# Exponents of the gated DeltaNet from one stacked product, one lane transpose for four, and the low halves of 22 weight tiles made a stage earlier and kept in DRAM

## The chip, the cores and the metric

The kernel runs on one core of one Trainium2 chip. The metric is device time in microseconds, the median of several executions. The engines are PE (TensorE: matmuls, and transposes as matmuls), DVE (VectorE), ACT (ScalarE), POOL (GpSimd) and SP, whose queue issues every DMA of this kernel. PEld is the loading of PE's stationary operand.

## The reference

Two layers over 256 latent and 256 context tokens of width 1024. Layer 0 mixes tokens with an RG-LRU block, layer 1 with a gated DeltaNet; a SwiGLU feed-forward part follows each. Every part is normed and modulated by six vectors made from `silu(c) @ ada_w`. Cut to the DeltaNet step, which is where most of the change lies (the kernel takes chunks of 128 tokens where this takes 64):

```python
def step(s, xs):
    qc, kc, vc, gc, bc = xs
    gc = jnp.cumsum(gc, axis=-1)
    diff = gc[..., :, None] - gc[..., None, :]
    decay = jnp.where(incl, jnp.exp(jnp.where(incl, diff, 0.0)), 0.0)
    kb = kc * bc[..., None]
    m = jnp.where(strict, jnp.einsum('bhid,bhjd->bhij', kb, kc) * decay, 0.0)
    rhs = jnp.concatenate([vc * bc[..., None], kb * jnp.exp(gc)[..., None]], axis=-1)
    sol = lax.linalg.triangular_solve(m, rhs, left_side=True, lower=True, unit_diagonal=True)
    ...
    attn = jnp.where(incl, jnp.einsum('bhid,bhjd->bhij', qc, kc) * decay, 0.0)
```

It runs for 16 value heads (8 key heads, each used by two), in two directions, over context and latents. `decay` is a 128x128 matrix for each chunk, direction and head: exp of a difference of two running sums. The projections `h @ w_in` in front of it are products with 49 weight tiles of 128 columns (8 q, 8 k, 16 v, 16 z and one of small rows).

## The kernel before

**Products.** A weight tile (128x1024 floats, 512 KB) is loaded into `raw` (three buffers), rounded to a high half `whi`, and what is left over becomes the low half `wlo` (two buffers each): `weight` (L704). A product (`product`, L943) is then three matmuls for each of 8 contraction tiles: high by high, high by low of the input, low by high. The copy to `whi` goes to ACT or DVE, the subtraction that makes `wlo` to DVE or POOL; inside the DeltaNet stage, until the z tiles, the subtraction is given to POOL alone. So a tile is 24 matmuls, 512 columns wide with both token sets.

**Stages.** In order: the RG-LRU part (to about 240 us of the profile), the feed-forward part of layer 0 (`ffn`, L1099, about 240 to 640), the DeltaNet (about 640 to 1130 with its output product, `ps_wo`), the feed-forward part of layer 1. In the first feed-forward part a background list `cur["bg"]` makes the modulation vectors of layer 1: each `bg_step` (L781) records one step, which loads a 512 KB tile into one of two `ring` slots and adds it on DVE to `acc`. `product` records one such step each time.

**DeltaNet.** Heads are taken in four groups of two key heads (four value heads), numbered 0 to 3. `stage_a` (A) projects one key head: k, two v tiles, q. For a group, `stage_e` (E) makes the exponents (`exponents`, L1275) and their exp, the 32 decay matrices of the tile `gn`; `stage_n` (N) multiplies them by k k^T, transposes the four 32x32 diagonal blocks into lanes (L1417) and inverts them there in a loop of 60 dependent DVE operations (`lmul`, `lw`); `stage_l` (L) assembles the whole inverse with small matmuls (`ps_w`, `ps_z`); `stage_p` (P) makes the attention matrices `at`, with exponents of its own (`ps_a`); `stage_c` (C) runs the chunks. Z makes the z tiles, W the output product that can start early.

An exponent tile of 128x512 (four heads) is a sum in one PSUM bank of three matmuls: a column term, whose stationary operand `cT` has 64 rows and whose moving operand `pick` is a broadcast; a row term (`rows`, `own`), and a mask (`below`, `identr`). In `stage_p` the column term of the second direction has 128 rows instead (`npick`, `rT`). There are 8 such tiles in each E and 4 in each P: 48 in all.

**Order.** Nothing is issued in the order of the code. A recorder collects the operations of a stage and `flush` (L391) places them with a list scheduler: every operation has a priority (its place in the record plus a bias), costs and latencies written in the source, and buffers are granted as they come free. The DeltaNet's record follows the table `PROG` (L73), its biases `TUNE["bias"]`. Each engine then runs its own list strictly in order, SP's list of DMAs included: a DMA whose buffer is not free holds back every DMA behind it. PE matmuls of any stage may stand between others.

Of the kernel before, what the change touches and what calls it, by code (L numbers as in the profile page):

```python
# [42 lines left out]
def _shuffle(sh, pattern, sizes):  # L43
# [18 lines left out]
    for g, n in zip(lhs, sh.shape, strict=True):  # L62
# [3 lines left out]
        for a in g:  # L66
# [6 lines left out]
PROG = "A0 A1 E0 A2 N0 A3 E1 L0 P0 N1 C0 A4 A5 E2 P1 L1 N2 C1 A6 Z0 A7 E3 L2 P2 N3 Z1 C2 Z2 Z3 L3 W0 P3 C3"  # L73
TUNE = dict(warm=5000, ev=3000, stay=(300, 0), g0=4, early=(1, 2, 4, 6), eb=0, ea=(0, 1, 1, 1), nwo=2, prog=PROG,
            bias={'C3': -1500, 'N0': 100, 'N': -700, 'Z3': -1200, 'L': -1500, 'E3': 700, 'W': 10000, 'L3': -800, 'E': -300, 'W0': 10000, 'P': -100, 'E0': -300, 'N3': -700, 'P2': 0, 'C': 400, 'A': 700, 'Z': 700, 'C1': 0})
# [545 lines left out]
def hybrid_block(ctx: ExitStack, tc: tile.TileContext, I, out, dbg=None):  # L621
# [82 lines left out]
    def weight(*src, cols=1024, aside=False, place=None):  # L704
# [29 lines left out]
    def ada_steps(l, m, direct=False):  # L734
# [41 lines left out]
        yield  # L776

# [165 lines left out]
    def product(src, n_k, xs, n, wmap=lambda w, k: w[:, 128 * k:128 * k + 128]):  # L943
        wh, wl = early.pop(0) if early else weight(src)
# [154 lines left out]
    def ffn(l, n, upd, hh, hl, first=None):  # L1099
# [32 lines left out]
    ada_later(1, 0, 1, 2, 3, 4, 5)  # L1132
# [114 lines left out]
    id64 = piece(64)  # L1247
    V.tensor_tensor(id64, ident[:, 0:64], ident[:, 64:128], OP.add)
    npick = dn.tile([128, 64], F32R, name="npick")
    V.tensor_scalar(npick, id64, -1.0, None, OP.mult)  # L1250
    pick = dn.tile([128, 32], F32R, name="pick")
    V.tensor_tensor(pick[0:64], ident[0:64, 0:32], ident[0:64, 32:64], OP.add)
    mod4 = piece(4)
    V.tensor_reduce(out=mod4, in_=ident.rearrange("p (m h) -> p h m", h=4), axis=AX.X, op=OP.add)
    own = {}
    for sign in (1, -1):
        own[sign] = dn.tile([128, 16], F32R, name=f"own{sign + 1}")
        t = piece(16)
        V.tensor_reduce(out=t, in_=id64.rearrange("p (i h) -> p i h", h=4), axis=AX.X, op=OP.add)
        V.tensor_scalar(own[sign], t, float(sign), None, OP.mult)  # L1260
    gch = dn.tile([128, 2, 2, 4, 16], F32R, name="gch")
    for d in range(2):
        R.copy(gch[:, d, 0], gc[:, :, d, :])
        V.tensor_tensor(gch[:, d, 1], gc[:, :, d, :], gch[:, d, 0].bitcast(F32), OP.subtract)
    pt = bank("tr", "ps_gt")
    for d in range(2):
        T.transpose(pt[:, 128 * d:128 * d + 128], gch[:, d].rearrange("p a c h -> p (a c h)").bitcast(F32), ident)
    rT = dn.tile([128, 2, 128], F32R, name="rT")
    R.copy(rT, pt[:, 0:256].rearrange("p (d i) -> p d i", d=2))
    rows = []  # L1270
    for d in range(2):
        rows.append(dn.tile([128, 4, 128], F32R, name=f"rows{d}"))
        V.tensor_tensor(rows[d], rT[:, d].bitcast(F32).rearrange("p (o i) -> p o i", o=1).to_broadcast([128, 4, 128]),
                        mod4.rearrange("p (h o) -> p h o", o=1).to_broadcast([128, 4, 128]), OP.mult)
# [35 lines left out]
    def stage_a(h):  # L1310
        a = A[h] = {}

        ps = product(I["dn_w_in"][8 + h], NK, hx1, 512) if h else ps_k0
# [18 lines left out]
        for j in range(2):  # L1332
            ps = product(I["dn_w_in"][16 + 2 * h + j], NK, hx1, 512)
# [23 lines left out]
    def stage_e(g):  # L1357
# [14 lines left out]
        cb = dn.tile([128, 2, 32], F32R, tag="cb", bufs=2, name="cb")  # L1372
        lf = lb.rearrange("p c d h -> p (c d h)")
        V.tensor_copy(cb[:, 0], lf)
        V.tensor_tensor(cb[:, 1], lf, cb[:, 0].bitcast(F32), OP.subtract)
        pt = bank("tr", "ps_cb")
        T.transpose(pt[0:64, 0:128], cb.rearrange("p a s -> p (a s)").bitcast(F32), ident)
        cT = t["cT"] = dn.tile([128, 128], F32R, tag="cT", bufs=2, name="cT")
        V.tensor_copy(cT[0:64], pt[0:64, 0:128])
        for c in range(4):  # L1380
            for d in range(2):
                s = sidx(c, d, 0)
                p4 = exponents(g, c, d, (1, -1)[d], 1, column(t, c, d), [gn])
                S.activation(gn[:, s:s + 4, :], p4, AF.Exp)

    def column(t, c, d):
        return t["cT"][0:64], pick[0:64, 4 * (2 * c + d):4 * (2 * c + d) + 4], 64

    def stage_n(g):
# [138 lines left out]
    def stage_p(g):  # L1528
# [3 lines left out]
        for c in range(2):  # L1532
            for d in range(2):
                col = (rT[:, 1], npick[:, 16 * (2 + c) + 4 * g:16 * (2 + c) + 4 * g + 4], 128) if d else column(t, 2 + c, 0)
                p4 = exponents(g, 2 + c, d, 1, (1, -1)[d], col, t["at"], "ps_a")
                for q in range(2):
                    S.activation(t["at"][q][:, c, d], p4[:, 2 * q:2 * q + 2], AF.Exp)
# [296 lines left out]
```

## Time and profile before

| | |
|---|---|
| median of 3 executions | 1363.38 us (1362.26 to 1370.28) |
| profiled execution: its time, its span | 1364.68 us, 1363.0 us |
| mean granted TensorE clock | 0.976 |
| PE busy, PEld busy | 1308.6 us, 1110.3 us |
| DVE, ACT, POOL busy | 1035.0, 564.9, 229.6 us |
| DMA moved, mean rate | 195.60 MB, 144 GB/s |

A row of the profile names what an instruction writes and reads (`ps_mm<-hh,whi`: the PSUM bank `ps_mm` from the operands `hh` and `whi`). All calls pass one helper, so all rows have line L612 and are told apart by these names. Matmuls are pipelined: the duration of one is longer than its distance to the next, so PE's real price for a matmul is the distance between the starts of neighbours. Instructions of PE in float32 (not in the rounded form) leave two records each.

### The profile page before, as it was taken

The page shows a single profiled execution, that of the slowest core. Times are in us where ns is not written, and L with a number is a line of the kernel's source. Part 1 is how long each engine was busy: PE and PEld are TensorE (multiplying, and loading weights), DVE is VectorE, ACT ScalarE, POOL GpSimd, SP SyncE. Part 2 cuts the span into 40 slices and gives each one's busy share as a digit, 9 for nine tenths or more (in the row PEclk, how much of TensorE's full clock was granted, in tenths as well). Part 3 has the DMA queues.
Part 4 walks back from the last instruction along what each step waited for, and adds up shares of the span by engine and source line. Part 5 has one row for each costly group of instructions (what it writes and reads, how often), then busy time and mean ns, then how long its engine had stood idle before and what let it go on. Part 6 is the DMA issues. An engine that isn't in the chain of part 4 may idle for free.

```text
span 1363.0 us, 23260 instructions
## 1 busy us (share of the span) xinstructions
PE 1308.6 (96%) x9200; PEld 1110.3 (81%) x9200; DVE 1035.0 (76%) x1851; ACT 564.9 (41%) x1053; POOL 229.6 (17%) x203
## 2 busy tenths in 40 slices
PE   5999999899999999999998999999998998999997
PEld 3677778878888888888867788898798888999997
DVE  5799986988775665557868889798499376877775
ACT  3388773444321111005746656747646431211100
POOL 2000000110100001212524333334243100000000
PEclk9899999899999999999999999999999699999999
DMA  9545423365564665333523222323133025455563
GB/s 352 197 165 188 140 94 114 124 202 196 188 228 164 192 208 183 98 110 125 178 74 129 71 78 79 105 71 121 63 117 117 25 92 180 139 182 180 179 181 116
DMA packets 61261, 195.60 MB, mean 144 GB/s; under 512 B 6752, under 2 KB 9952, under 8 KB 60896
## 3 DMA queue, kind: packets, MB, share of 16 engines
q1 hardware_dynamic: 61152, 194.12, 42.8%
q8 instruction: 72, 1.18, 0.4%
q14 instruction: 37, 0.30, 0.1%
HBM read 184.13 MB, written 9.96 MB: 142 GB/s over the span
## 4 chain that ended last, share of the span: by engine, by line
PE 56%; issue 15%; DVE 6%; ACT 4%; DMA 1%; POOL 0%; POOLq 0%; SPq 0%; ACTq 0%; DVEq 0%
PE ps_mm L612 29%; PE ps_dn L612 9%; PE ps_e L612 2%; PE ps_wo L612 2%; PE ps_y L612 2%; PE ps_w L612 2%; PE ps_z L612 2%; PE ps_s L612 1%; DVE lw L612 1%; PE ps_ks L612 1%; DVE cu L612 1%; PE ps_a L612 1%; PE ps_qs L612 1%; PE ps_o L612 1%; ACT gn L612 1%
## 5 line engine op out<-in xcount | busy, mean ns | idle before, releaser
L612 PE MATMUL ps_mm<-hh,whi 128*128 128x512 f32 (+1 forms) x888 | 327.4, 370 | 8.0 <-DVE cu L612 5.6
L612 PE MATMUL ps_mm<-hl,whi 128*128 128x512 f32 (+1 forms) x888 | 327.3, 370 | 0.9 <-DVE hl L612 0.8
L612 PE MATMUL ps_mm<-hh,wlo 128*128 128x512 f32 (+1 forms) x888 | 326.2, 368 | 1.7 <-POOL wlo L612 1.7
L612 DVE TENSOR_TENSOR wlo<-raw,whi 128x1024 fp32r<-128x1024 f32 (+2 forms) x183 | 220.5, 1205 | 17.4 <-ACT whi L612 8.3
L612 DVE CAST whi<-raw 128x1024 fp32r<-128x1024 f32 (+2 forms) x177 | 120.2, 679 | 145.8 <-PE ps_mm L612 81.0
L612 POOL TENSOR_TENSOR wlo<-raw,whi 128x1024 fp32r<-128x1024 f32 x55 | 132.0, 2402 | 506.5 <-DVE whi L612 351.3
L612 PEld LDWEIGHTS ps_mm<-hh,whi 128*128 128x128 f32 x888 | 169.6, 191 | 40.6 <-issue 9.9
L612 PEld LDWEIGHTS ps_mm<-hh,wlo 128*128 128x128 f32 x888 | 169.7, 191 | 29.6 <-POOL wlo L612 2.4
L612 PEld LDWEIGHTS ps_mm<-hl,whi 128*128 128x128 f32 x888 | 170.0, 192 | 27.4 <-DVE hl L612 2.0
L612 PE MATMUL ps_dn<-fh,wlo 128*128 128x256 f32 (+1 forms) x374 | 122.7, 328 | 0.0
L612 PE MATMUL ps_dn<-fl,whi 128*128 128x256 f32 (+1 forms) x374 | 122.5, 327 | 0.0
L612 PE MATMUL ps_dn<-fh,whi 128*128 128x256 f32 (+1 forms) x374 | 122.2, 327 | 0.0
L612 PE MATMUL ps_mm<-h2h,whi 128*128 128x256 f32 x352 | 100.4, 286 | 1.1 <-ACT h2h L612 1.1
L612 PE MATMUL ps_mm<-h2l,whi 128*128 128x256 f32 x352 | 100.6, 286 | 0.5 <-DVE h2l L612 0.3
L612 PE MATMUL ps_mm<-h2h,wlo 128*128 128x256 f32 x352 | 100.1, 284 | 0.0
L612 ACT ACTIVATE whi<-raw 128x1024 fp32r<-128x1024 f32 (+2 forms) x61 | 63.2, 1036 | 77.8 <-PE ps_mm L612 45.1
L612 ACT ACTIVATE fh<-sg 128x256 fp32r<-128x256 f32 (+1 forms) x43 | 22.4, 522 | 156.4 <-DVE sg L612 156.3
L612 ACT ACT_TABLE_LOAD x59 | 75.7, 1283 | 7.0 <-DMA sm<-small 3.4
L612 PEld LDWEIGHTS ps_dn<-fl,whi 128*128 128x128 f32 x374 | 71.1, 190 | 6.4 <-issue 0.4
L612 PEld LDWEIGHTS ps_dn<-fh,wlo 128*128 128x128 f32 x374 | 71.1, 190 | 6.4 <-issue 0.4
L612 PEld LDWEIGHTS ps_dn<-fh,whi 128*128 128x128 f32 x374 | 71.1, 190 | 6.0
L612 DVE SCALAR_TENSOR_TENSOR x<-ring,cs,x 128x1024 f32<-128x1024 f32 x49 | 63.9, 1304 | 15.4 <-DMA ring<-ada_w 14.4
(326 smaller groups left out, 2544.7 us busy)
## 6 DMA issues: line engine op xcount, KB each, us to landing
ring<-ada_w SPq DMA_DIRECT2D x96, 512.0 KB, 4.5
raw<-ffn_gu SPq DMA_DIRECT2D x88, 512.0 KB, 3.5
raw<-dn_w_in SPq DMA_DIRECT2D x49, 512.0 KB, 3.5
raw<-ffn_down SPq DMA_DIRECT2D x34, 512.0 KB, 3.6
raw<-rg_w_in SPq DMA_DIRECT2D x16, 512.0 KB, 4.5
raw<-ffn_down SPq DMA_DIRECT2D x17, 384.0 KB, 3.4
raw<-dn_w_out SPq DMA_DIRECT2D x12, 512.0 KB, 3.6
raw<-rg_w_out SPq DMA_DIRECT2D x10, 512.0 KB, 3.4
```

Source lines behind the costliest of these rows:

```text
L612: call(*[real(x) for x in args], **{n: real(v) for n, v in kw.items()})
```

## The change

**Stacked exponents.** The column and the row term become one matmul. For each group a tile `src` holds, side by side, high and low halves of the running sums, ones, and the column logarithms; three transposes put them on partitions (`ps_src`), and DVE multiplies them into two operands by masks of zeros and ones (`spread`): `X` (four heads, 128x512, shared by all exponents of the group) and `Y` (eight chunk and direction pairs, 128x1024), with `Y2` (128x256) for the second direction of P. An exponent tile is then X by one block of Y, and the mask: two matmuls, both over 128 rows. `X`, `Y`, `Y2` and `src` have one buffer each, so the next group's E writes them after this group's P has read them. The old operands (`cT`, `rows`, `own`, `npick`, `rT`) go.

**One lane transpose.** Four copies on ACT gather the diagonal blocks into `lc` (32 partitions by 1024 each), and one DVE transpose of 128x1024 takes the place of four of 32x1024.

**Low parts in DRAM.** `low_steps` adds 22 background steps in the feed-forward part of layer 0, between the second and the third modulation vector of layer 1. Each loads one k or v tile of the DeltaNet into a `ring` slot, rounds it on ACT, subtracts (DVE or POOL), and writes the 512 KB of low half to DRAM. For these tiles `weight` later makes only `whi`; `wlo` is loaded from DRAM. The feed-forward loop records one more background step in every second round.

**Order.** `PROG` moves P before the next E and some other entries; the bias of L goes from -1500 to -2200.

On PE, the first two exponent tiles of group 0 before, with the products around them (`ps_e` the exponents, `ps_mm` a projection):

```order
L612 MATMUL ps_mm<-hh,whi 128x512
L612 MATMUL ps_e<-pick,cT 128x512
L612 MATMUL ps_e<-rows_5410,own_5116 128x512
L612 MATMUL ps_e<-below,identr 128x512
L612 MATMUL ps_mm<-hl,whi 128x512
L612 MATMUL ps_e<-pick,cT 128x512
L612 MATMUL ps_e<-rows_5417,own_5118 128x512
L612 MATMUL ps_e<-below,identr 128x512
```

The same place now (`ex` is X, `ey` is Y):

```order
L612 MATMUL ps_mm<-hh,whi 128x512
L612 MATMUL ps_e<-ex,ey 128x512
L612 MATMUL ps_e<-below,identr 128x512
L612 MATMUL ps_mm<-hl,whi 128x512
L612 MATMUL ps_e<-ex,ey 128x512
L612 MATMUL ps_e<-below,identr 128x512
```

One matmul of three has gone from each tile, and none of those left works on 64 rows.

On SP, in the feed-forward part of layer 0, a stretch before (`raw<-ffn_gu` is the next product's weight tile, `ring` the background's):

```order
L612 DMA raw<-ffn_gu 128x1024
L612 DMA ring<-ada_w 128x1024
L612 DMA raw<-ffn_gu 128x1024
L612 DMA ring<-ada_w 128x1024
L612 DMA raw<-ffn_gu 128x1024
L612 DMA ring<-ada_w 128x1024 x2
L612 DMA raw<-ffn_gu 128x1024
```

And a stretch now, while the low parts are made:

```order
L612 DMA low<-ring 128x1024 x2
L612 DMA ring<-dn_w_in 128x1024
L612 DMA raw<-ffn_gu 128x1024
L612 DMA ring<-dn_w_in 128x1024
L612 DMA raw<-ffn_gu 128x1024
L612 DMA low<-ring 128x1024 x2
L612 DMA ring<-dn_w_in 128x1024
L612 DMA raw<-ffn_gu 128x1024
```

There are eleven such pairs of writes, most with this pattern after them: two loads of the ring and two weight tiles between one pair and the next. Each ring load needs the write that empties its slot to have landed, and a weight tile stands behind it.

On DVE, the lane transposes of group 0 before, between the convolutions (`cu`) of a projection:

```order
L612 STREAM_TRANSPOSE lw<-gn 32x1024
L612 SCALAR_TENSOR_TENSOR cu<-ps_mm,sm,cu 128x2x254
L612 STREAM_TRANSPOSE lw<-gn 32x1024
L612 SCALAR_TENSOR_TENSOR cu<-ps_mm,sm,cu 128x2x255
L612 TENSOR_SCALAR cu<-ps_mm,sm 128x512
L612 SCALAR_TENSOR_TENSOR cu<-ps_mm,sm,cu 128x2x255
L612 SCALAR_TENSOR_TENSOR cu<-ps_mm,sm,cu 128x2x254
L612 STREAM_TRANSPOSE lw<-gn 32x1024
```

And now:

```order
L612 SCALAR_TENSOR_TENSOR cu<-ps_mm,sm,cu 128x2x255
L612 TENSOR_SCALAR cu<-ps_mm,sm 128x256
L612 STREAM_TRANSPOSE lw<-lc 128x1024
L612 SCALAR_TENSOR_TENSOR cu<-ps_mm,sm,cu 128x254
L612 MEMSET lw 128x32
```

One transpose stands where four stood, and the convolutions are no longer parted by several of them.

```diff
-PROG = "A0 A1 E0 A2 N0 A3 E1 L0 P0 N1 C0 A4 A5 E2 P1 L1 N2 C1 A6 Z0 A7 E3 L2 P2 N3 Z1 C2 Z2 Z3 L3 W0 P3 C3"
+PROG = "A0 A1 E0 A2 N0 A3 P0 E1 L0 N1 A4 A5 C0 P1 E2 L1 N2 C1 A6 Z0 A7 P2 E3 L2 Z1 N3 C2 Z2 Z3 L3 W0 P3 C3"
...
     def weight(*src, cols=1024, aside=False, place=None, low=None):
         r = raws.pop(0) if raws else raw_load(src, cols)
         hi, lo = place or (wp.tile([128, 1024], F32R, tag=t, bufs=NB[t], name=t) for t in ("whi", "wlo"))
+        if low is not None:
+            R.copy(hi, r)
+            sync.dma_start(out=lo.bitcast(F32), in_=low)
+            return hi, lo
...
+    def low_steps(tiles):
+        low = dr.tile([len(tiles), 128, 1024], F32, name="low")
+        for n, i in enumerate(tiles):
+            r, hi = next(cur["araw"]), cur["acc"][:, 1]
+            sync.dma_start(out=r, in_=I["dn_w_in"][i], after=cur["late"])
+            S.activation(hi.bitcast(F32R), r, AF.Copy)
+            R.tt(r.bitcast(F32R), r, hi, OP.subtract)
+            sync.dma_start(out=low[n], in_=r)
+            LOW[i] = low[n]
+            yield
...
+                bg_step(l == 0 and j % 2)
...
-    ada_later(1, 0, 1, 2, 3, 4, 5)
+    ada_later(1, 0, 1)
+    cur["bg"].append(low_steps([i for h in range(NQK) for i in (8 + h, 16 + 2 * h, 17 + 2 * h)][2:2 + TUNE["low"]]))
+    ada_later(1, 2, 3, 4, 5)
...
-    def exponents(g, c, d, sign, bound, col, to, name="ps_e"):
-        ps = bank("tr", name)
-        p4 = ps.rearrange("p (h i) -> p h i", h=4)
-        i = 4 * c + g
-        lhs, rhs, n = col
-        T.matmul(p4, lhs, rhs.rearrange("p (h o) -> p h o", o=1).to_broadcast([n, 4, 128]), start=True, stop=False, needs=to)
-        T.matmul(p4, own[sign][:, i:i + 1].to_broadcast([128, 128]), rows[d], start=False, stop=False)
+    def exponents(lhs, rhs, bound, to, name):
+        p4 = bank("tr", name).rearrange("p (h i) -> p h i", h=4)
+        T.matmul(p4, lhs, rhs, start=True, stop=False, needs=to)
         lhs, rhs = (identr, below) if bound > 0 else (below, identr)
         T.matmul(p4, lhs, rhs.rearrange("p (o i) -> p o i", o=1).to_broadcast([128, 4, 128]), start=False, stop=True)
...
+        for k, i in enumerate((0, 1, 3)):
+            T.transpose(pt[:, 128 * k:128 * k + 128], src[:, i:i + 2].rearrange("p a x -> p (a x)").bitcast(F32), ident,
+                        needs=[X, Y, Y2])
+        spread(X, pt[:, 0:128], mod4, 4)
+        spread(Y, pt[:, 128:256], own, 8)
+        spread(Y2, pt[:, 256:384], own2, 2)
...
+        lc = dn.tile([128, 32, 32], F32, tag="lane", bufs=3, name="lc")
         w = dn.tile([128, 32, 32], F32, tag="lane", bufs=3, name="lw")
         for b in range(4):
             r = slice(32 * b, 32 * b + 32)
-            V.transpose(w[r], gn[r, :, 32 * b:32 * b + 32].rearrange("p s f -> p f s"))
+            S.activation(lc[r], gn[r, :, 32 * b:32 * b + 32], AF.Copy)
+        V.transpose(w, lc.rearrange("p s f -> p f s"))
```

More of the change, by code (lines that the diff above doesn't have):

```diff
@@ L702, in raw_load, with weight @@
         return r
-    def weight(*src, cols=1024, aside=False, place=None):
+    def weight(*src, cols=1024, aside=False, place=None, low=None):
         r = raws.pop(0) if raws else raw_load(src, cols)
         hi, lo = place or (wp.tile([128, 1024], F32R, tag=t, bufs=NB[t], name=t) for t in ("whi", "wlo"))
+        if low is not None:
+            R.copy(hi, r)
+            sync.dma_start(out=lo.bitcast(F32), in_=low)
+            return hi, lo
         if aside:
@@ L776, in ada_steps @@
         yield
+    LOW = {}
+    def low_steps(tiles):
[8 more added lines that the diff above has]
+            yield
     def ada_later(l, *ms, direct=False):
@@ L941, in hybrid_block, with product @@
     ol = m0.tile([128, NK, 512], F32R, name="ol", tag="ol", bufs=1)
-    def product(src, n_k, xs, n, wmap=lambda w, k: w[:, 128 * k:128 * k + 128]):
-        wh, wl = early.pop(0) if early else weight(src)
+    def product(src, n_k, xs, n, wmap=lambda w, k: w[:, 128 * k:128 * k + 128], low=None):
+        wh, wl = early.pop(0) if early else weight(src, low=low)
         bg_step()
@@ L1246, in hybrid_block @@
     R.copy(identr, ident)
[L1247 to L1253, printed above, removed]
-    V.tensor_reduce(out=mod4, in_=ident.rearrange("p (m h) -> p h m", h=4), axis=AX.X, op=OP.add)
[L1255 to L1274, printed above, removed]
-    def exponents(g, c, d, sign, bound, col, to, name="ps_e"):
-        ps = bank("tr", name)
-        p4 = ps.rearrange("p (h i) -> p h i", h=4)
-        i = 4 * c + g
-        lhs, rhs, n = col
-        T.matmul(p4, lhs, rhs.rearrange("p (h o) -> p h o", o=1).to_broadcast([n, 4, 128]), start=True, stop=False, needs=to)
-        T.matmul(p4, own[sign][:, i:i + 1].to_broadcast([128, 128]), rows[d], start=False, stop=False)
+    sel = dn.tile([128, 14], F32, name="rowsel")
@@ new lines, in hybrid_block @@
+    mod4, own, own2 = sel[:, 0:4], sel[:, 4:12], sel[:, 12:14]
+    V.tensor_reduce(out=mod4, in_=ident.rearrange("p (m h) -> p h m", h=4), axis=AX.X, op=OP.add)
+    mod32 = piece(32)
+    V.tensor_reduce(out=mod32, in_=ident.rearrange("p (m h) -> p m h", h=4), axis=AX.X, op=OP.add)
+    V.tensor_reduce(out=own, in_=mod32.rearrange("p (x i) -> p i x", i=8), axis=AX.X, op=OP.add)
+    V.tensor_scalar(own[0:64, 1:8:2], own[0:64, 1:8:2], -1.0, None, OP.mult)
+    V.tensor_scalar(own2, own[:, 5:8:2], -1.0, None, OP.mult)
@@ L1283, in exponents, with spread @@
+    def spread(out, part, mask, n):
+        V.tensor_tensor(out, part.rearrange("p (o i) -> p o i", o=1).to_broadcast([128, n, 128]),
+                        mask.rearrange("p (n o) -> p n o", o=1).to_broadcast([128, n, 128]), OP.mult)
+    def exponents(lhs, rhs, bound, to, name):
+        p4 = bank("tr", name).rearrange("p (h i) -> p h i", h=4)
+        T.matmul(p4, lhs, rhs, start=True, stop=False, needs=to)
         lhs, rhs = (identr, below) if bound > 0 else (below, identr)
@@ L1311, in stage_a @@
         a = A[h] = {}
-        ps = product(I["dn_w_in"][8 + h], NK, hx1, 512) if h else ps_k0
+        ps = product(I["dn_w_in"][8 + h], NK, hx1, 512, low=LOW.get(8 + h)) if h else ps_k0
         kT = a["kT"] = dn.tile([128, 512], F32, tag="kT", bufs=8, name="kT")
@@ L1332, in stage_a @@
         for j in range(2):
-            ps = product(I["dn_w_in"][16 + 2 * h + j], NK, hx1, 512)
+            ps = product(I["dn_w_in"][16 + 2 * h + j], NK, hx1, 512, low=LOW.get(16 + 2 * h + j))
             v2 = conv_silu(ps, 16 + 2 * h + j, 2)
@@ L1382, in stage_e @@
                 s = sidx(c, d, 0)
[L1383 to L1387, printed above, removed]
+                S.activation(gn[:, s:s + 4, :], exponents(Y[:, 2 * c + d], X, 1, [gn], "ps_e"), AF.Exp)
     def stage_n(g):
@@ L1533, in stage_p @@
             for d in range(2):
-                col = (rT[:, 1], npick[:, 16 * (2 + c) + 4 * g:16 * (2 + c) + 4 * g + 4], 128) if d else column(t, 2 + c, 0)
-                p4 = exponents(g, 2 + c, d, 1, (1, -1)[d], col, t["at"], "ps_a")
+                lhs = t["Y2"][:, c] if d else t["Y"][:, 4 + 2 * c]
+                p4 = exponents(lhs, t["X"], (1, -1)[d], t["at"], "ps_a")
                 for q in range(2):
```

25 lines of the change are left out of this document (16 added, 9 removed).

## The prediction

> **What bounds the kernel now.** I read the page's busy shares and chain of waits first.
>
> ```profile
> span 1363.0 us, 23260 instructions
> PE 1308.6 (96%) x9200; PEld 1110.3 (81%) x9200; DVE 1035.0 (76%) x1851; ACT 564.9 (41%) x1053; POOL 229.6 (17%) x203
> PE 56%; issue 15%; DVE 6%; ACT 4%; DMA 1%; POOL 0%; POOLq 0%; SPq 0%; ACTq 0%; DVEq 0%
> ```
>
> PE is busy nearly throughout and the chain of what ended last lies mostly on it; POOL and SP's queue hold none. Next I took the table of busy times by stretch, for the feed-forward part (240 to 640 us), the DeltaNet (640 to 1130), and places in it.
>
> ```profile
> core 0: us, PE busy (x) PEld busy (x) DVE busy (x) ACT busy (x) POOL busy (x), PEclk, DMA share, GB/s
> 0.00:25.00 25.00, 12.93 (x72) 8.15 (x72) 11.70 (x32) 7.88 (x20) 3.20 (x20) 1.00 0.91 331
> 240.00:640.00 400.00, 394.67 (x1942) 328.56 (x1941) 279.66 (x351) 102.34 (x155) 45.37 (x28) 0.99 0.52 170
> 640.00:1130.00 490.00, 470.52 (x4292) 401.21 (x4290) 387.01 (x921) 288.86 (x614) 164.70 (x135) 0.97 0.29 96
> 710.00:720.00 10.00, 5.16 (x30) 4.46 (x30) 9.87 (x14) 3.74 (x5) 4.76 (x2) 0.93 0.26 87
> 850.00:950.00 100.00, 98.05 (x1073) 85.57 (x1072) 88.45 (x196) 63.35 (x138) 39.13 (x38) 1.00 0.30 101
> 1050.00:1075.00 25.00, 22.49 (x419) 20.13 (x417) 9.89 (x15) 14.32 (x28) 5.81 (x5) 0.56 0.17 54
> ```
>
> Both long stretches are PE's: 394.67 of 400 us and 470.52 of 490. In the DeltaNet DVE is second with 79%, up to 88% between 850 and 950; ACT and POOL have room. So PE's own work there is worth time until DVE takes over.
>
> **The exponents.** The timeline of PE at the first exponents of group 0 gives start and duration of each matmul:
>
> ```profile
> 682.65 0.48 PE L612 MATMUL ps_e<-pick,cT 64*128 64x512 f32 x1
> 683.06 0.50 PE L612 MATMUL ps_e<-rows,own 128*128 128x512 f32 x1
> 683.40 0.40 PE L612 MATMUL ps_e<-below,identr 128*128 128x512 f32 x1
> 683.73 0.48 PE L612 MATMUL ps_e<-pick,cT 64*128 64x512 f32 x1
> ...
> 684.48 0.40 PE L612 MATMUL ps_e<-below,identr 128*128 128x512 f32 x1
> 684.71 0.39 PE L612 MATMUL ps_mm<-hh,wlo 128*128 128x512 f32 x1
> 684.94 0.40 PE L612 MATMUL ps_mm<-hh,whi 128*128 128x512 f32 x1
> ...
> 675.28 0.28 PE L612 MATMUL ps_mm<-hh,wlo 128*128 128x256 f32 x1
> 675.40 0.28 PE L612 MATMUL ps_mm<-hh,whi 128*128 128x256 f32 x1
> ...
> 675.64 0.38 PE L612 MATMUL ps_a<-npick,rT 128*128 128x512 f32 x1
> 675.86 0.28 PE L612 MATMUL ps_mm<-hh,wlo 128*128 128x256 f32 x1
> 675.97 0.39 PE L612 MATMUL ps_a<-rows,own 128*128 128x512 f32 x1
> 676.20 0.28 PE L612 MATMUL ps_mm<-hh,whi 128*128 128x256 f32 x1
> ```
>
> A tile with `pick` takes 683.73 - 682.65 = 1.08 us from start to start; a plain 512-column matmul takes 684.94 - 684.71 = 0.23, the mask too (684.71 - 684.48). The surplus of 0.4 us sits at the change between 64 and 128 rows: after `npick`, which has 128 rows, the same two steps take 0.22 and 0.23. X and Y have 128 rows, so I price the new tile as two plain matmuls, 0.46. Counts: 32 tiles in E and 8 in P lose 1.08 - 0.46 = 0.62 each, 24.8 us; 8 tiles in P lose the 0.22 of `npick`, 1.8 us. Sum 26.6. The other end is that only the streaming goes: 48 x 0.23 = 11.0. I take 26.6, since the `npick` rows show the plain price in the same place.
>
> The Trainium skill speaks of a lower price: "TensorE: Matmul & The Clock Gate", section "Back-to-back issue gap", gives about 131 ns per 512-column matmul in a sustained stream. By it 48 matmuls would be an estimated 6 us; the rows here show 0.23 us for a plain one and more at a change of rows.
>
> New on PE are 12 transposes of 128x128 for six of the old kernel. Rows for transposes, copies and subtractions, from the groups by form and the answer for one tile:
>
> ```profile
> L612 PE MATMUL ps_vt<-ident,cu x64: 271/273/332, 652.8 to 958.6; 128*128 128x128 f32 x64
> L612 DVE STREAM_TRANSPOSE lw<-gn 32x1024 f32<-32x1024 f32 x16 | 32.0, 2001 | 0.3
> L612 DVE STREAM_TRANSPOSE ld<-lw 128x1024 f32<-128x1024 f32 x4 | 8.2, 2050 | 0.1
> L612 DVE TENSOR_TENSOR at<-ps_kq,at 128x512 f32<-128x512 f32 x16 | 10.3, 679 | 0.2 <-PE ps_kq L612 0.2
> L612 DVE TENSOR_TENSOR wlo<-raw,whi 128x1024 fp32r<-128x1024 f32 x162 | 201.5, 1244 | 14.7 <-ACT whi L612 7.2
> L612 ACT ACTIVATE whi<-raw 128x1024 fp32r<-128x1024 f32 x57 | 60.3, 1057 | 73.7 <-PE ps_mm L612 45.1 <-issue 17.2 <-PE ps_dn L612 7.6
> L612 POOL TENSOR_TENSOR wlo<-raw,whi 128x1024 fp32r<-128x1024 f32 x55 | 132.0, 2402 | 506.5 <-DVE whi L612 351.3 <-ACT whi L612 104.4 <-PE ps_mm L612 28.2
> ```
>
> Six more at 0.27 at most: +1.6; pipelined they are nearer to +0.7. I take +1.
>
> **The spreads and the lane transpose.** A spread has no row. The nearest is `at<-ps_kq,at`, two operands with one in PSUM, 0.68 us for 512 elements; X, Y and Y2 are 1792, so 3.5 x 0.68 = 2.4 us a group, 9.5 in all. Sixteen lane transposes of 2.00 us go (32.0) and four of 2.05 come (8.2): a transpose costs the same on 32 partitions as on 128. DVE in the DeltaNet has 32.0 - 8.2 - 9.5 = 14.3 us less, the small operations that leave and come taken as equal. ACT gets 16 copies of 1024 elements, at 1.06 each 17 us, on 289 of 490: hidden. On a path that ends something stands only the N of group 3, where its L and C follow with little else for PE: 4 x 2.0 = 8.0 us become 4 x 1.06 + 2.05 = 6.3. Bounds -3 and +3 (ACT's copies queue behind others); I take -1. In group 0 the row of 710 to 720 shows PE at 5.16 of 10 while DVE is full: those 4.8 us could shrink, and I put them in a rival, not in the sum, since what DVE does next there is the convolution, which stays.
>
> **The low parts, in the feed-forward part.** Per tile: a ring load, an ACT copy (1.06), a subtraction (1.24 on DVE), a 512 KB write. 22 of them are 23 us of ACT on 102 of 400 and 27 us of DVE on 280, covered by PE's 394.67. The traffic rises by 23 MB on 400 us, 58 GB/s on 170; 331 were moved in the first stretch. What can fail is the pace of the ring. From the DMA views (time to landing, medians; the first three rows of 240 to 640, the others of 640 to 1130 and of the whole):
>
> ```profile
> ring<-ada_w SPq DMA_DIRECT2D x56, 512.0 KB, 4.4
> raw<-ffn_gu SPq DMA_DIRECT2D x41, 512.0 KB, 3.7
> x2d<-x SPq DMA_DIRECT2D x1, 1024.0 KB, 3.8
> vspill<-vp SPq DMA_DIRECT2D x16, 256.0 KB, 2.1
> raw<-dn_w_in SPq DMA_DIRECT2D x44, 512.0 KB, 3.5
> x<-xT SPq DMA_DIRECT2D x2, 512.0 KB, 9.3
> ```
>
> A 512 KB write lies between 2.1 and 3.8, say 2.9. A slot then turns over in 4.4 + 1.06 + 1.24 + 2.9, with some 0.4 for four handovers: 10.0 us, and both slots do so side by side. SP's order lets two weight tiles through per pair; PE uses two in 48 x 0.23 = 11.0. The pace holds with 1.0 us to spare, and weight tiles are loaded up to three ahead, 16 us of PE. So this part costs 0; the bounds are 0 and what the fourth rival works out.
>
> **The low parts, in the DeltaNet.** POOL loses 22 x 2.40 = 53 us of 165, which ended nothing. `whi` is still made. In exchange `wlo` is a load that waits at the head of SP's queue until PE releases the buffer; the next weight tile, the spills of k and v and their reloads stand behind it. It lands 3.5 us after the release. Behind a k or v product PE has another tile (24 x 0.23 = 5.5 us) to go on with; behind the second v comes q, with 24 matmuls at 256 columns, 0.12 each by the starts at 675.28 and 675.40, 2.9 us. The k tile after it can be 3.5 - 2.9 + 0.3 = 0.9 late, seven times: 0 to 6 us. I take +2, since exponents and chunk products mostly stand between.
>
> **Sum.** -26.6 + 1 - 1 + 0 + 2 = -24.6, on the profiled execution's 1364.68: 1340.1. The median of the runs is 1.3 below that execution, so 1339 to 1340; I predict 1340.
>
> **The rivals.**
> 1. *DVE becomes the bound.* For it: 88.45 of 100 between 850 and 950; E now ends in spreads that the next group's E can only write after P has read X. Against it: DVE's own work falls too. Then the gain is DVE's 14.3 us less about 3 of E's longer start: 1364.7 - 11 = 1353. It decides where DVE is full for a stretch and PE's rows show waits for DVE. Chance 0.16.
> 2. *Only streaming is saved* (the change of rows is paid elsewhere, or X by Y is no faster): 11.0 - 2 = 9 us, 1355. The `npick` rows speak against it. Chance 0.05.
> 3. *The clock.* In the row of 1050 to 1075, where L stands nearly alone with its small matmuls, the granted clock is 0.56 though PE is busy for 22.49 us; earlier L's, with 512-column matmuls among them, keep 1.00. If one more L is left alone, about 25 x 0.44 = 11 us come back: 1351. Chance 0.04. The Trainium skill's "TensorE: Matmul & The Clock Gate", section "What's actually happening", says the clock halves after an idle window of about 3.4 us. By that rule this stretch, busy at 90%, should not have dropped; the row shows that busy time alone does not keep the clock.
> 4. *The ring starves the feed-forward part (slower).* If loads land as under the first stretch's traffic (9.3), writes in 3.8 and the subtraction waits for one more of DVE's (1.24), a pair takes 9.3 + 1.06 + 2.48 + 3.8 + 0.4 = 17.0. SP's weight loads behind it come 6.0 us late per pair, 66 over eleven pairs, less 16 that were loaded ahead: +50, and 1390. It begins to cost above 11.0 + 16/11 = 12.5 us per pair and eats the whole gain at 14.7. Against it: 4.4 in this very stretch. Chance 0.07.
> 5. *More than forecast:* the waits of 710 to 720 and the like go with the transposes, and POOL's relief helps the rest: -32, 1332. Chance 0.12.
>
> The forecast itself has 0.56, with its own range 1334 to 1347. From the median 1%, about what a measurement of this kernel can tell from no change, is 13.6 us: faster means below 1349.7. That holds for the forecast, the fifth rival and a fifth of the first: 0.71. The others of the first three lie within 1%: 0.22. Slower: 0.07. For the range I leave out half of the fifth rival below and the fourth with part of the second above: 1329 to 1356.
>
> **What would show it.** In the changed profile: two `ps_e` rows per tile, 0.46 us from start to start where they stand together, 64 and 32 rows of `ps_e` and `ps_a` in place of 96 and 48; the DeltaNet's stretch from the first `ps_ba` to the last `ps_wo` shorter by about 25; PE full (25 of 25) in every stretch of the feed-forward part, with landings of ring and `low` near 4.4 and 2.9; four transposes of about 2.05 us; few waits of PE for `wlo`. I am wrong if the feed-forward part grows (then it is the ring), if the DeltaNet shrinks by less than 15 while `ps_e` keeps 0.46 (then DVE or the order), or if the pairs of `ps_e` stay near 0.7 (then the price).

## The result, and the profile after

The changed kernel takes 1374.57 us (median of 18 executions, 1366.98 to 1383.49), the kernel before 1362.36 beside it (18 executions, 1354.28 to 1370.28): a ratio of 1.0095, with a 95% interval of 1.0072 to 1.0118. It is 12 us slower; the forecast, 1340, lay some 23 us below the kernel before. Executions of one kernel differ by some 16 us, and each trace shows one of them: that of after is one of the shorter ones, 1367.9 us, 3 us above that of before.

The page of after, in the same lines as of before:

```profile
span 1366.1 us, 23391 instructions
PE 1299.7 (95%) x9158; PEld 1116.7 (82%) x9158; DVE 1051.5 (77%) x1892; ACT 602.5 (44%) x1081; POOL 167.4 (12%) x182
issue 15%; PE 9%; DVE 3%; ACT 2%; DMA 1%; POOL 0%; POOLq 0%; SPq 0%; ACTq 0%; DVEq 0%
```

The chain of waits accounts for only 30% of the span here, so I read stretches instead. The table of busy times by stretch, for after:

```profile
core 0: us, PE busy (x) PEld busy (x) DVE busy (x) ACT busy (x) POOL busy (x), PEclk, DMA share, GB/s
240.00:640.00 400.00, 390.51 (x1896) 323.78 (x1897) 297.43 (x359) 126.67 (x176) 38.10 (x26) 0.98 0.66 225
640.00:1130.00 490.00, 460.90 (x4261) 407.39 (x4261) 378.17 (x943) 299.41 (x613) 105.74 (x114) 0.95 0.35 119
850.00:875.00 25.00, 20.73 (x442) 19.15 (x441) 18.04 (x34) 17.53 (x39) 11.86 (x9) 0.86 0.41 129
975.00:1000.00 25.00, 22.35 (x305) 20.58 (x306) 8.81 (x15) 11.88 (x20) 0.95 (x1) 0.68 0.14 44
1050.00:1075.00 25.00, 20.53 (x418) 18.55 (x417) 10.98 (x19) 15.58 (x30) 5.46 (x6) 0.61 0.16 55
```

And of before, the stretches in which L1 and L2 run there (L1 stands in the first of them in both kernels, L2 in the second of before and the 975 to 1000 of after):

```profile
850.00:875.00 25.00, 23.93 (x428) 19.68 (x427) 18.87 (x38) 20.30 (x42) 8.29 (x8) 1.00 0.26 90
945.00:970.00 25.00, 22.25 (x504) 19.68 (x503) 16.46 (x37) 21.39 (x41) 10.12 (x8) 1.00 0.26 88
```

In the DeltaNet PE is 10 us less busy than before (460.90 against 470.52), and its granted clock fell from 0.97 to 0.95. The stretches of L1 and L2, which kept a clock of 1.00, now have 0.86 and 0.68. The stage itself, by the rows of its first and last tile (columns: count, durations in ns, first and last start), first before, then after:

```profile
L612 PE MATMUL ps_ba<-ident,baT x4: 222/222/271, 641.1 to 641.4; 64*128 64x64 f32 x4
L612 PE MATMUL ps_wo<-oh,wlo x128: 276/283/582, 1047.4 to 1152.5; 128*128 128x256 f32 x128
```

```profile
L612 PE MATMUL ps_ba<-ident,baT x4: 222/222/272, 645.4 to 645.6; 64*128 64x64 f32 x4
L612 PE MATMUL ps_wo<-oh,wlo x128: 278/283/582, 1048.1 to 1155.4; 128*128 128x256 f32 x128
```

It lasts 1152.5 - 641.1 = 511.4 us before and 1155.4 - 645.4 = 510.0 after. It begins 4.3 us later; what follows it is as long as it was. So the added 3 us of this execution lie ahead of the DeltaNet, and the forecast gain of 25 in it shrank to 1.4.

The 4.3 us understate what the change costs there. From the first `sg<-ps_mm` of the feed-forward part to the first `ps_ba` the traces take 379.7 us before and 388.2 after, 8.5 us more. But this execution of after came to that first row 4.3 us sooner (257.1 against 261.4), at the end of the RG-LRU part, which the change leaves alone; over all traces that row starts between 257.1 and 264.0, with low parts or without. The twelve kernels without low parts take 379.2 to 379.8 us from the one row to the other, the eight with them 388.2 to 391.9.

The price of the exponents is not the reason. PE's timeline of after at group 0:

```profile
688.67 0.40 PE L612 MATMUL ps_mm<-hl,whi 128*128 128x512 f32 x1
688.90 0.39 PE L612 MATMUL ps_e<-ex,ey 128*128 128x512 f32 x1
689.13 0.39 PE L612 MATMUL ps_e<-below,identr 128*128 128x512 f32 x1
689.36 0.39 PE L612 MATMUL ps_mm<-hh,wlo 128*128 128x512 f32 x1
```

Two steps of 0.23, 0.46 us per tile, as forecast. I therefore took the DeltaNet's matmul records apart. For every pair of neighbours of like shapes I took the median distance of their starts at full clock, over all traces below. The sum of these medians is the *work* of PE. What a matmul takes beyond it at half clock is *half clock*; every surplus above 0.45 us is a *wait*; the *rest* is small surpluses. In us, from profiled executions:

```
kernel                          stage   work   half clock   waits   rest
before                          511.4  441.9      14.2       21.6   33.6
after                           510.0  420.3      24.4       32.1   33.3
e5  exponents cut, old order    500.9  408.8      15.3       37.8   38.9
e6  half of the N loops         510.3  441.9      13.9       20.8   33.7
e1  low parts alone             515.1  441.2      16.1       23.8   33.9
e14 the same, thin ring loads   514.0  441.2      13.1       23.1   36.6
e11 after, mask twice           518.0  431.3      23.0       30.2   33.4
other order, work as before:
e3  one lane transpose          519.7  442.5      13.1       27.1   37.0
e12 program and L bias of after 530.5  440.6      20.2       36.5   33.2
e13 L bias of after             523.1  441.6      19.6       26.2   35.7
e15 lane copy, other buffer     526.8  440.9      20.4       27.5   37.9
e17 A bias                      526.5  440.4      17.4       35.2   33.6
e8  L bias, a little            513.4  442.5      13.6       25.5   31.9
e18 C bias                      512.4  442.0      10.1       25.0   35.4
stacked exponents, other edits:
e2  no low parts                525.2  420.0      29.9       43.2   32.2
e4  E2 brought forward          520.0  421.0      27.8       36.2   35.0
e9  exponents alone             528.8  420.5      27.3       48.4   32.6
e10 after without lane          529.0  420.1      33.2       45.6   30.0
e16 after, old L bias           516.4  420.8      29.0       33.1   33.5
```

After has 21.6 us less work than before. Of these, 10.2 came back as streaming at half clock and 10.5 as waits. Each row is one execution, so a few us between two rows mean little by themselves. The experiments ask whether that is the nature of the stage or the doing of the order that came with the change.

### The profile page after: what moved, and what is told of

Read it like the earlier page. It is cut to its first block, busy times and chain, and to the rows that moved or that the text cites. A ratio compares the mean times of both kernels' runs of the same rounds, so it can differ in the third digit from the quotient of the medians.

```text
span 1366.1 us, 23391 instructions
## 1 busy us (share of the span) xinstructions
PE 1299.7 (95%) x9158; PEld 1116.7 (82%) x9158; DVE 1051.5 (77%) x1892; ACT 602.5 (44%) x1081; POOL 167.4 (12%) x182
## 5 line engine op out<-in xcount | busy, mean ns | idle before, releaser
L612 DVE CAST whi<-raw 128x1024 fp32r<-128x1024 f32 (+2 forms) x169 | 116.5, 689 | 135.5 <-PE ps_mm L612 81.2
L612 POOL TENSOR_TENSOR wlo<-raw,whi 128x1024 fp32r<-128x1024 f32 x31 | 78.0, 2519 | 575.1 <-DVE whi L612 433.4
L612 ACT ACTIVATE whi<-raw 128x1024 fp32r<-128x1024 f32 (+2 forms) x69 | 70.2, 1019 | 108.7 <-PE ps_dn L612 48.3
```

Source lines behind the costliest of these rows:

```text
L612: call(*[real(x) for x in args], **{n: real(v) for n, v in kw.items()})
```

## The experiments

All were timed in three rounds, with the kernel before beside them (its medians 1359.99 to 1365.72). A ratio is to before, with its 95% interval; that of after is 1.0095.

### The parts one at a time

Three theories stood at first. **Theory A**: the DeltaNet is a serial chain of N and L, and PE merely fills it. **Rival B**: DVE's whole work bounds it. **Rival C**: the loads of `wlo` hold it up.

*e1: before with the low parts alone.*

> The kernel before with the low parts alone (22 background steps, wlo of those tiles from DRAM); old exponents, four lane transposes, old order table. Theory A (the DeltaNet is a serial chain of N and L, and the low parts cost what the feed-forward part and the first tiles of the DeltaNet lose): slower than before by 5 to 12 us, the feed-forward part 4 to 8 us longer. Rival B (DVE's total work is the bound): POOL's relief does not touch DVE, so within 3 us of before. Rival C (the loads of wlo hold up the DeltaNet): slower by 15 us or more, nearly all of it after the first DeltaNet product.

Measured 1377.37 us, 1.0099 (1.0061 to 1.0137). In its trace the DeltaNet is 3.7 us longer than before; from the first `sg<-ps_mm` to the first `ps_ba` it takes 391.9 us, 12.2 more. So nearly all of the loss lies ahead of the DeltaNet.

*e2: after without the low parts.*

> The changed kernel without the low parts: stacked exponents, one lane transpose and the new table stay. Theory A: the 5 to 12 us of the low parts come back, and since E of group 2 then stands ahead of L of group 1 in PE's order, N of group 2 starts up to 20 us earlier: 1343 to 1362. Rival B: 1370 or more, as the DVE work of the DeltaNet is the same as in the changed kernel. Rival C: 1350 or less.

1376.85, 1.0088 (1.0059 to 1.0116).

*e3: before with the one lane transpose alone.*

> The kernel before with the one lane transpose alone (16 copies more on ACT, 24 us less on DVE). Theory A: only the N of group 3, which waits for its exponents and nothing else, gains, about 2 us: within 5 us of before. Rival B: DVE's 24 us show, 15 to 24 us faster than before.

1375.94, 1.0091 (1.0062 to 1.0120).

*e4: after with E2 brought forward*, since in after its first `ps_e` starts at 884.5, behind L1, and before at 837.3:

```diff
-'E0': -300,
+'E0': -300, 'E2': -3500,
```

> The changed kernel with one more entry in the table of biases, so that E of group 2 is placed ahead of L of group 1, as in the kernel before. Nothing else differs. Theory A: N of group 2 starts right behind L of group 1, about 20 us earlier than in the changed kernel, and the end moves by 12 to 20 us: 1354 to 1363. Rivals B and C: same as the changed kernel, 1374 within 4.

1379.60, 1.0103 (1.0072 to 1.0135). E2 did move (its first `ps_e` starts at 860.7, ahead of L1), and the 12 to 20 us of theory A did not come. So the low parts alone and the lane transpose alone each cost what all parts cost together, and taking the low parts away mends nothing. No theory foresaw e3: an edit that takes 24 us off DVE costs 12. C falls with e1, where the loss lies ahead of the DeltaNet, and with e2, where these loads of `wlo` are gone. What e1 cost there is taken up with e14.

### PE, or DVE

In the next three, the planner places every instruction as it would, and the ones named are left out only at the issue; so the order of all others stays word for word that of the kernel they come from. The edits are shown by what is then issued. **Theory O**: PE is the bound, and after lost its gain by the order it was given.

*e5: before, of each exponent's three matmuls only the mask is issued.*

```diff
-        T.matmul(p4, lhs, rhs.rearrange("p (h o) -> p h o", o=1).to_broadcast([n, 4, 128]), start=True, stop=False, needs=to)
-        T.matmul(p4, own[sign][:, i:i + 1].to_broadcast([128, 128]), rows[d], start=False, stop=False)
...
-        T.matmul(p4, lhs, rhs.rearrange("p (o i) -> p o i", o=1).to_broadcast([128, 4, 128]), start=False, stop=True)
+        T.matmul(p4, lhs, rhs.rearrange("p (o i) -> p o i", o=1).to_broadcast([128, 4, 128]), start=True, stop=True)
```

> The kernel before, with two of the three matmuls of each exponent (48 x 2 of 0.23 us, and the changes between 64-row and 128-row tiles with them) left out; every other instruction stands in the very order of the kernel before on every engine, and nothing on DVE, ACT, POOL or the queues changes. The exponents are then all masked, so the decays come out as zeros; the work behind them keeps its size. Theory A (DeltaNet is a serial chain of N and L on DVE, PE only fills it): the 22 to 26 us of PE work come out as waits, the time changes by less than 7 us. The theory of the prediction (PE is the bound there, what it loses the stage loses): 18 to 26 us faster, about 1340. Theory O (PE is the bound under a good order, and the kernel after lost the gain by the order it was given): as the prediction, about 1340, since this order is the old one.

1353.51, 0.9938 (0.9920 to 0.9957): 8 us faster. By the table the work fell by 33.1 and the stage by 10.5; 16.2 came back as waits and 5.3 in the rest. Neither side has it: in its old order PE's time counts, at a quarter of its price (8 us of 33). Waits of PE in e5, 640 to 1160 us (us in total, times, longest):

```profile
PE ps_kt L612 <- ACT kT L612: 5.8, 3, 4.5
PE ps_mm L612 <- DVE cu L612: 5.7, 3, 3.1
PE ps_e L612 <- ACT gn L612: 3.4, 4, 2.0
```

PE arrives earlier at the same places, and there waits for the exponentials and convolutions that ACT and DVE still have to finish. The second row stood at 5.6 before; the `kT` row at 1.3, and the `gn` row is new.

*e6: before, with every second step of the N loops left out.*

```diff
-        for c in range(1, 31):
+        for c in range(2, 31, 2):
```

> The kernel before in its own order with every second step of the four N loops left out (odd steps; 2 DVE instructions each, about 10 us of DVE in each of the four loops), so the inverses are not the reference's. Theory A: the loop lies on the chain, 25 to 40 us faster, about 1330. PE as the bound: at most 8 us faster. Theory O does not need either.

1365.20, 1.0010 (0.9991 to 1.0030): nothing. The DeltaNet by stretch, before and then e6:

```profile
640.00:1160.00 520.00, 495.69 (x4474) 425.39 (x4473) 408.77 (x954) 292.38 (x622) 165.41 (x136) 0.97 0.30 99
```

```profile
640.00:1160.00 520.00, 495.73 (x4487) 426.78 (x4486) 379.67 (x834) 291.62 (x621) 163.72 (x136) 0.97 0.29 99
```

DVE lost 29 us, PE did not move. *e7: the same cut in after.*

> The kernel after in its own order with the same half of the four N loops left out. Theory A: 25 to 40 us faster than after (1374), about 1340. Theory O (after has turned PE work into waits for a late E): 10 to 25 us faster. PE as the bound: at most 8 us.

1371.49, 1.0063 (1.0040 to 1.0086), some 4 us less than after's ratio, and the intervals overlap. Theory A, my first reading of the traces, falls with e6 and e7: the loops are not what the stage waits for. Rival B falls with e6, where 29 us less of DVE bring nothing.

### The order

*e8: before with the bias of L moved from -1500 to -1600*, which shuffles the order a little and changes no instruction's work.

> The kernel before with one number of the planner's table moved (L from -1500 to -1600): the same instructions, in an order that differs a little in DeltaNet. It measures what a change of order alone is worth. Theory A and O: a few us either way, 1360 to 1380. If it comes to 1363 within 2 us, the order is no cause of differences of 12 us.

1364.05, 1.0020 (1.0004 to 1.0035). This change of order costs little. By the words above it would have cleared the order of a difference of 12 us; the runs below show that one small shuffle is no test of that. From here on, **Theory K**: PE bounds the stage, what it is relieved of comes back as waits and half clock, and the lane transpose costs by itself, through its buffer. **Rival R**: the order that the stacked exponents force is what loses.

*e9: the stacked exponents alone (old lane transposes, no low parts).*

> The kernel after without the low parts and with the old four transposes of 32 rows: the stacked exponents alone, with the program of stages that they need. Theory K (PE bounds DeltaNet; of the PE time that the exponents free, about half comes back as waits of PE, half as streaming at half clock; the lane transpose costs by itself, since its copy takes a second of the three lane buffers, which come free only as the L before it ends): without the lane transpose some 12 us less than the run with both, 1358 to 1370. Rival R (the order that the stacked exponents force, P before the next E, is what loses): 1372 to 1380, the lane transpose then costs nothing beside it.

1380.69, 1.0104 (1.0069 to 1.0139). *e10: after with the old lane transposes.*

> The kernel after with the old four transposes of 32 rows in place of copies and one lane transpose: exponents and low parts stay. Theory K: 8 to 15 us faster than after (1374), 1359 to 1367. Rival R: within 4 us of after.

1390.35, 1.0175 (1.0109 to 1.0241). *e12: before with the program of stages and the bias of L of after.*

```diff
-PROG = "A0 A1 E0 A2 N0 A3 E1 L0 P0 N1 C0 A4 A5 E2 P1 L1 N2 C1 A6 Z0 A7 E3 L2 P2 N3 Z1 C2 Z2 Z3 L3 W0 P3 C3"
+PROG = "A0 A1 E0 A2 N0 A3 P0 E1 L0 N1 A4 A5 C0 P1 E2 L1 N2 C1 A6 Z0 A7 P2 E3 L2 Z1 N3 C2 Z2 Z3 L3 W0 P3 C3"
...
-'L': -1500,
+'L': -2200,
```

> The kernel before with the stage program and the bias of L of after (P0 ahead of E1, P2 ahead of E3, C0 behind A5; L -2200), and with every instruction as before: the new order of stages alone. Rival R: 8 to 15 us slower than before, 1371 to 1378. Theory K: within 5 us of before (1363).

1381.92, 1.0129 (1.0089 to 1.0168): 16 us slower with the instructions of before. e9 and e12 speak for R, a little beyond its numbers. e10 fits neither: R said no difference to after, K a gain, and it is 11 us above after's ratio. Its four executions stand far apart (1384 to 1399), and its interval meets that of after at the edge. The same lane transpose costs 12 us in the old order (e3), saves some 11 in that of after (e10) and 2 where the low parts are left out (e2 against e9), so what it costs is not its own price. In e12's waits of PE (640 to 1160) one row tops the list:

```profile
PE ps_ks L612 <- DVE S L612: 8.4, 2, 6.7
```

PE stands for 6.7 us at one product of a chunk for a state `S` that DVE, which runs its list in order, had placed late. The row is not among PE's waits of before.

*e13: the bias of L alone, in before.*

> The kernel before with the bias of L at -2200 as in after, the stage program left as it was. The run with both (program and bias) came out 16 us above before. If the bias carries it: 1372 to 1380. If the program of stages (P ahead of the next E) carries it: 1360 to 1368.

1372.92, 1.0097 (1.0059 to 1.0135). *e16: the old bias of L, in after.*

> The kernel after with the bias of L back at -1500, the program of stages and all the rest as in after. If the bias is what loses there: 1355 to 1366. If it is the program: 1370 to 1385.

1377.83, 1.0136 (1.0108 to 1.0164). So the bias alone costs before 13 us, and taking it back from after mends nothing: it is not that one number. *e15: the lane transpose alone, but its copy in the buffer of `xo`*, to take away the second lane buffer:

```diff
-        lc = dn.tile([128, 32, 32], F32, tag="lane", bufs=3, name="lc")
+        lc = dn.tile([128, 32, 32], F32, tag="xo", bufs=1, name="lc")
```

> The kernel before with the one lane transpose alone, but the copy takes the buffer of xo and lmul and not one of the three lane buffers. If the lane transpose alone was 12 us slower since its copy holds a second lane buffer: 1360 to 1368. If it is the order that comes out, or the four copies on ACT: 1372 or more.

1376.21, 1.0125 (1.0095 to 1.0155): the buffer was not it. The last two move other numbers of the same table, in before: *e17, the bias of A from 700 to 900*, and *e18, that of C from 400 to 600.*

> The kernel before with the bias of A moved from 700 to 900: no instruction's work changes, the planner deals out another order in DeltaNet (the lane transpose alone, the bias of L alone and the program alone each came 12 to 16 us above before). If the order of before is an uncommonly good one and any large change of order loses what a common order costs: 1369 to 1382. If those three orders were bad for reasons of their own: 1357 to 1367.

> The kernel before with the bias of C moved from 400 to 600: a smaller change of order on DVE and ACT (a quarter as many rows as with A). If the order of before is uncommonly good: 1363 to 1376. If not: 1357 to 1364.

e17: 1378.33, 1.0118 (1.0076 to 1.0161). e18: 1363.23, 1.0018 (0.9997 to 1.0038). In e17 the waits of PE are led by another chunk product:

```profile
PE ps_y L612 <- DVE r L612: 11.8, 3, 7.4
```

Seven kernels now differ from before only in order (e3 and e15 by the lane transpose too, which gives DVE time back). Five are 12 to 17 us slower, two within 3 us, none is faster. Their work on PE is the same to 2 us; in the five the stage grew by 8 to 19 us, in waits, half clock and rest. By these seven the order of before is an uncommonly good one, and five of the changes cost some 15 us, whatever the edit was. Why these five lose and e8 and e18 do not is not shown beyond the late products above.

### What PE's time is worth in the new order

*e11: after, in its own order, with each mask matmul issued twice.*

> The kernel after in its own order, with the mask matmul of each exponent issued twice: 48 matmuls of 0.23 us of full-size PE work put back, 11 us, nothing else moved; the values stay the reference's. If PE time counts in full in after: 11 us slower, about 1385. Theory K: they stand largely in waits and keep the clock up, 0 to 5 us slower, 1374 to 1380, with a granted clock nearer to that of before (0.970 against 0.964). Rival R says as K, or 11.

1380.27, 1.0114 (1.0076 to 1.0151): 0.0019 above after's ratio, 3 us for 11 us of PE work, though the intervals would allow from none to all of it. In the two traces its stage is 8.0 us longer, but that of after is a short execution, so this run alone does not settle it. The mean granted clock of its executions is 0.969, that of after's 0.964. The stages agree across kernels: five in another order with the old exponents (e3, e12, e13, e15, e17) average 525.3 us, the six with stacked ones (after, e2, e4, e9, e10, e16) 521.6. Some 21 us of work less show as 4. Best against best says no more: before, the shortest with the old exponents and all their work, has 511.4, and after, the shortest of the six, 510.0.

### The low parts

*e14: e1, in its order, with the ring loads cut to an eighth of their size.*

```diff
-            sync.dma_start(out=r, in_=I["dn_w_in"][i], after=cur["late"])
+            sync.dma_start(out=r[:, 0:128], in_=I["dn_w_in"][i][:, 0:128], after=cur["late"])
```

> The run with low parts alone, every instruction in the same order, but each of the 22 loads of a weight tile into the ring brings only an eighth of its columns (64 KB in place of 512 KB), so the low parts are not the reference's. If what the low parts cost in the feed-forward part is the pace of their transfers (DMA share 0.81 against 0.58 there, DVE waits 20 us for the ring): at least 5 of the 14 us come back, 1364 to 1372. If it is the place of the added steps on ACT, DVE and the queue: within 3 us of it, 1374 to 1380.

1375.02, 1.0112 (1.0085 to 1.0138), as e1; from the first `sg<-ps_mm` to the first `ps_ba` it takes 391.0 us, e1 391.9. The DMA issues of e14 show the cut (KB each, us to landing):

```profile
low<-ring SPq DMA_DIRECT2D x22, 512.0 KB, 3.0
ring<-dn_w_in SPq DMA_DIRECT2D x22, 64.0 KB, 2.7
```

So it is not the pace of the ring loads; the writes to DRAM were left as they are. From the first `ps_dn` to the first `ps_ba` PE takes 143.4 us before, and 143.1 to 143.4 in e13, e15, e17 and e18; with low parts 153.6 (after), 154.2 (e1) and 153.7 (e14). The added steps stand between those of the modulation vectors, two of which (`ps_ada`) move from the products into this stretch. There PE, in order, waits for DVE's part of the step. The timeline of e1:

```profile
520.51 1.08 PE L612 MATMUL ps_ada<-x,sel 128*32 128x256 f32 x8 [3.45 <-DVE x L612]
```

Between 500 and 640 us PE's busy time (second number) is 138.13 of 140 us before, 133.29 in after and 133.72 in e14. In after PE's waits there are led by that for DVE's `x` (3.9 us) and one for ACT's `sq` (2.2 us), neither of which before has. That the place of the added steps costs this, and not the pace of the writes, is argued from these waits: no run left the writes out. The lines, before, after and e14:

```profile
500.00:640.00 140.00, 138.13 (x727) 118.04 (x726) 84.50 (x126) 23.36 (x47) 24.65 (x18) 0.99 0.44 140
```

```profile
500.00:640.00 140.00, 133.29 (x702) 112.36 (x701) 100.13 (x133) 29.32 (x51) 17.69 (x17) 0.98 0.62 206
```

```profile
500.00:640.00 140.00, 133.72 (x691) 112.10 (x690) 98.12 (x124) 27.61 (x47) 17.69 (x15) 0.98 0.65 214
```

No run beat the kernel before, save e5, which leaves work out.

## Why the prediction was wrong

Two steps of the sum failed: the DeltaNet gave 1.4 us in the traces where the sum has 24.6, and the feed-forward part, put at 0, cost 8.5.

**The exponents on PE, -26.6.** The price was right (0.46 us a tile) and the work did go: 21.6 us net of the new transposes, where the prediction had 25.6. What failed is the sentence ahead of it, "PE's own work there is worth time until DVE takes over": I took a PE that is busy 96% of the stage for one whose every microsecond ends the stage. In the old order 33.1 us off PE gave 8 us (e5). PE's list is strict, and behind each place where it arrives early stands a wait for DVE or ACT that its own work had covered. Busy shares cannot tell such a cover from a bound.

**The order, no term at all.** The prediction priced what instructions cost and not where they would stand; the new `PROG` and the bias of L got neither a term nor a rival, and the order is named only among the signs of being wrong. In the kernel before they alone cost 16 us (e12), more than the whole effect, and four other changes of this order cost 12 to 17. How much of that after pays is not shown: no run has its instructions in the order of before, and the parts do not add. Each alone costs 12 to 15 us, all together 12, and one pair (e10) 25.

**The low parts, 0 and +2.** The feed-forward part was not free: 8.5 us in after, 12.2 in e1. The pace of the ring held, as forecast, since landings stayed at 4.5 and 3.2 us where 4.4 and 2.9 were assumed. But the added work on DVE and ACT was taken as covered by a PE that is busy for 394.67 of 400 us, which again reads a busy share as a bound; PE waits in order for DVE's share of the shifted steps. In the DeltaNet the loads of `wlo` cost nothing to be seen: one wait of PE, of 0.2 us.

The 8.5 us and the 1.4 make 7 of the 12 us between the medians. The rest lies in executions that have no trace, and stays open.

**The lane transpose, -1.** The transposes cost as forecast (2.03 us where 2.05 was assumed; 32.0 us in all became 8.1), and DVE's relief was worth nothing, as e6 shows for the loops behind them. Nor did the copy wait for a lane buffer at a cost (e15).

**The rivals.** The slower one was right in sign and in its stage and wrong in its mechanism; thinner ring loads change nothing (e14). *Only streaming is saved* falls with the 0.46 us. *DVE becomes the bound* was half right: waits went to DVE and ACT, but to single late products, not to DVE's total. *The clock*, given 0.04, was right in kind and near in size: one more L left alone, 11 us back, it said. L2 is that L, at half clock from 983.8 to 1000.9, and half clock took 10.2 us more in the whole stage. It is one half of where the freed work went in the profiled execution. The range, to 1356, let the gain shrink but left no room for a cost of the order or of the feed-forward part.

## What to carry to other kernels

A kernel with a finely set order carries part of its speed in that order: before pricing an edit that changes it, reshuffle the old kernel several times with no edit at all, and take what that costs (here 2 to 17 us, five times of seven over 12) as the first term. Time taken off an engine that is 96% busy is worth only what its in-order waits let through; freeze the order, leave the instructions out, and measure that share (here a quarter) before building the edit. And when products move to other places, ask which small matmuls they kept warm.

## What the runs showed of the hardware

**The clock follows how much of the array is filled, not busy time.** The records give the granted clock in pieces that are multiples of 3.41 us. I cut the DeltaNet of the 19 traces in the table into such pieces and summed the columns that PE streamed in each, weighted by the part of the 128x128 array that a matmul uses. A record of a rounded matmul counts once; one of a transpose counts twice, and so does each of the two records of a float32 matmul, since at full clock records of both kinds with 128 columns start 0.11 us apart, nearly as far as rounded ones of 256 (0.12). Of pieces with under 2000, 205 of 207 were followed by half clock; between 2000 and 3500, 59 of 168; above 3500, none of 2492. The weight is not settled: the best single limit misplaces 42 of the 2867 pieces with it, 14 when only the rows of the array are counted, 154 with no weight, and 183 when busy time takes the place of columns.

L2 shows it. Between 945 and 970 us of before, at a clock of 1.00, 66 matmuls of projections (`ps_mm`) and no exponents stand among L2's. Between 984 and 1001 of after there is no projection; PE is busy for 16.40 of 17 us, and the clock is 0.50. So what L2 of after lacks is the projections and not the exponents: e5, without two thirds of the exponents' matmuls, keeps 1.00 in its L2. At half clock streaming takes twice the time. The same 128-column products in the timeline of before at full clock (six in 0.83 us) and in that of after at half clock (eight in 2.08 us):

```profile
966.95 0.83 PE L612 MATMUL ps_y<-vl,gn 128*128 128x128 f32 x6
```

```profile
987.66 2.08 PE L612 MATMUL ps_y<-vl,gn 128*128 128x128 f32 x8
```

The Trainium skill, "TensorE: Matmul & The Clock Gate", section "HAM oscillation — how this bites in real kernels", puts the cost of throttled time at half of it; the records agree, with 24.4 us lost in 48.6 (after) and 14.2 in 29.4 (before), waits left out. Its rule for avoiding it, no idle gaps of PE above some 3.4 us, is borne out once in after, where PE waits 4.2 us for DVE's `cu` until 855.6 and half clock runs from 854.1 to 860.9, just ahead of L1 (the 0.86 above). It is not enough here: of the 54.6 us at half clock in after's stage 37.6 lie in L2 and L3, in stretches where PE is busy for 89 and 82% of the time.

**The clock tells the two families of kernels apart.** Averaged over a kernel's executions the granted clock is 0.977 to 0.979 for before, 0.972 to 0.980 in every other kernel with the old exponents, and 0.960 to 0.969 with the stacked ones, without exception; single executions overlap. That the missing exponents themselves lower it is not shown: e5, which has even less of that work in the order of before, has 0.976.
